# First expert in a place of 64 slots, heavy places between light ones, HGRN heads in pairs, score products in turns

## The chip, the cores and the metric

The kernel runs on one core of a Trainium2 chip. The core has a matrix engine (TensorE, PE in the profile), three engines for elementwise work (VectorE is DVE, ScalarE is ACT, GpSimd is POOL), and SyncE (SP), on whose queue nearly all weight loads are issued. PEld in the profile is TensorE's loading of the stationary operand. The metric is the device time of one execution in microseconds; less is better.

## The reference, cut to what matters

Two transformer blocks run in series over 256 tokens of width 1024, all in float32. The first has a mixer of four differential-attention heads and eight neighbourhood-attention heads, and a mixture of 32 experts of which each token takes 4. The second has two layers: layer 0 mixes by retention and NSA (the even mixer), layer 1 by HGRN2 (the odd mixer), and a dense SwiGLU follows each.

```python
# first block
o_diff = diff_attention(dq, dk, dv, lam, lam_init, g_subln)     # 4 heads, two score maps each
o_nat = neighbourhood_attention(nq, nk, nv, nat_rpb)            # 8 heads
x = x + gt1 * rms_norm(concat(o_diff, o_nat) @ w_out, g_post_mix)
h2 = rms_norm(x, g_pre_ffn) * (1 + sc2) + sh2
top_val, top_idx = top_k(h2 @ w_router + b_router, 4)
gates = softmax(top_val)
for e in range(32):                       # only the tokens that chose e
    y[e] = swiglu_clamped(h2[tok[e]] @ w1[e] + b1[e]) @ w2[e] + b2[e]     # w1: 8 MB, w2: 4 MB
x = x + gt2 * rms_norm(sum of gates * y, g_post_ffn)
# second block
x = x + retention_nsa_mixer(rmsnorm(x));  x = x + swiglu(rmsnorm(x))
x = x + hgrn2_mixer(rmsnorm(x));          x = x + swiglu(rmsnorm(x))
# hgrn2, per head: S_t = diag(f_t) S_{t-1} + k_t v_t^T ; o_t = S_t^T q_t      (8 heads, chunks)
```

With the given inputs the routing sends 33 tokens to expert 0. The other experts, sorted by load, have 93, 75, 62, 61, then 48 and less, and from about the middle of the list 32 and less.

## The kernel before

**Stages.** The first mixer runs until about 190 us of the trace, the experts from there to about 1170, and the second block to the end: even mixer, dense layer, odd mixer, dense layer.

**Places.** `experts()` works through 32 places in turn. Place 0 always holds expert 0, whose weights can be loaded before the routing is known. The other experts are sorted by load on the chip: `route()` computes their ranks and the one-hot matrix `PM`, a matrix product turns it into the row `ids` (which expert stands in which place), and SP reads an id from it by a TENSOR_LOAD before it issues that expert's loads. The table `SLOTS` fixes how many token slots each place has: 128, 64 or 32. The heaviest experts go to the 128-slot places, the lightest to the 32-slot ones.

**Work of a place.** Each expert has 12 weight tiles of 128x2048 float32: eight of w1 (`w1(p, dc)`) and four of w2. In a place of 64 or 32 slots the tile goes into the products as it is. In a place of 128 slots `split_e` divides each half tile into a high part (`ehi`, on ACT) and a low part (`elo`, on DVE), three products are summed, and the tokens are split likewise (`Xh`, `Xl`). The tokens of several places are gathered together by one-hot products (`gather`, tiles `oh` and `X`), and results are scattered back with gates (`scatter`, tile `macc`). The first three w1 steps of place p+1 stand ahead of the w2 steps of place p.

**Buffers.** Expert tiles rotate through 13 buffers of 1 MB (`tile_e`): eight in the pool `wp`, which the mixer's weights use too, and five in the pool `wx`, which opens when the mixer's pools close. Two more tiles of expert 0 (`w0`) lie in borrowed space.

**Order.** In `first_ffn` the order on PE and SP is the order of the code (`manual_schedule`). SP issues its loads strictly in turn, and a load that waits for a buffer holds up all behind it. On the other engines, and on all engines in the mixers, a scheduler sets the order.

**Score products.** `scores()` and its like in NSA compute for each head pair four products of 64 rows: two heads in the upper and lower half of the partitions (m or g), and two query halves (qt). Neighbouring products from different halves of the array can run at the same time; where the scheduler put both products of one half in a row, they do not.

**Odd mixer.** Each of the eight heads projects q and f (48 products `acc<-hh,whi` and the like, L91), then works through levels L = 1, 2, ... 128. At each level there is one small group of products (`ps_t<-qk`, 32x32) and one DVE multiplication (L1428) of the tile `qk`. Then come the products with `ip` (`ps_t<-ip,at`), ScalarE's square sums, a root on POOL, and the scaled copy to `on` (L1459). The PSUM banks are two of each kind, `s` and `t`, in rotation.

Of the kernel before, what the change touches and what calls it, by code (L numbers as in the profile page):

```python
# [31 lines left out]
class Block:  # L32
# [57 lines left out]
    def mm(self, out, lhsT, rhs, start, stop=False):  # L90
        self.nc.tensor.matmul(out, lhsT, rhs, start=start, stop=stop, skip_group_check=True)  # L91
# [249 lines left out]
    def first_mixer(self):  # L341
# [9 lines left out]

        self.norm_T(evac)
# [31 lines left out]
        def tm(g, fill=lambda: None):  # L384
            t = att.tile([128, 2, 512], F32, name=f"v{g}")
# [13 lines left out]
        ali = att.tile([128, 4, 384], F32, name="ali")  # L399
        nc.sync.dma_start(ali, A["alibi"])  # L400
# [19 lines left out]
        gt1 = att.tile([128, D], F32, name="gt1")  # L420
        prow = att.tile([128, 2, 512], F32, name="prow")
# [6 lines left out]
        for h in range(4):  # L428
# [3 lines left out]
            for m in range(2):  # L432
                P = att.tile([128, 2, T], F32, name="P", tag="P", bufs=4)
                for qt in range(2):
                    self.softmax_unit(P[:, qt], sps[m][:, qt], ali[:, h, 128 * (1 - qt):128 * (1 - qt) + 256],
                                      rs[:, m, qt:qt + 1])
# [87 lines left out]
    def scores(self, q, k):  # L524

        sps = [self.bank("s").rearrange("p (a k) -> p a k", a=2) for _ in range(2)]
        for qt in range(2):
            for m in range(2):
                r = slice(m * 64, m * 64 + 64)
                self.mm(sps[m][:, qt], q[r, qt * 128:qt * 128 + 128], k[r], start=(qt == 0), stop=(qt == 1))  # L530
# [94 lines left out]
    def places(self):  # L625
# [14 lines left out]
        self.placed = nc.vector.tensor_scalar(PM, self.rankof, rank, None, op0=OP.is_equal)  # L640
# [5 lines left out]
        nc.vector.tensor_copy(self.ids, pi[0:1, :NE])  # L646
# [80 lines left out]
    def gather(self, ps):  # L727
# [10 lines left out]
        for p in ps:  # L738
# [3 lines left out]
            if w == 128:  # L742
                Xh = self.moe.tile([128, ND, 2 * CAP], F32R, name="Xh")
# [13 lines left out]
        def part(q):  # L757
# [6 lines left out]
            for j in range(2):  # L764
                dc = 2 * q + j
                nc.scalar.activation(X[:, dc, :n], acc[:, j * 256:j * 256 + n], AF.Identity,
                                     bias=self.sh2[:, dc:dc + 1], scale=self.s2[:, dc:dc + 1])
            if Xh is not None:
                d = slice(2 * q, 2 * q + 2)
                self.last_act = nc.scalar.copy(Xh[:, d], X[:, d, big])  # L770
# [10 lines left out]
    def slot(self, k):  # L781
        if k < 8:
            return self.wp.tile([128, 2048], F32, name="w")
        return self.wx.tile([128, 2048], F32, name="w", tag=f"w{k}")
# [107 lines left out]
    def first_ffn(self):  # L892
        self.scratch = lambda: self.moe.tile([128, D], F32, name="scr", tag="Xh")
# [653 lines left out]
    def run(self):  # L1547
# [7 lines left out]
        if self.stop == 1:  # L1555
            return
# [178 lines left out]
```

## Time and profile before

| what | value |
|---|---|
| median of three runs | 1874.76 us (1873.25 to 1874.95) |
| the profiled execution | 1873.16 us |
| its span in the trace | 1871.6 us |
| first mixer | 0 to about 190 us |
| experts | about 190 to 1170 us |
| second block | about 1180 us to the end |

The profile page gives the busy share of each engine over the whole span; these are averages over stages with different limits. To see what bounds a stage, read a view of windows: for a stretch it gives the busy time of each engine, the granted clock of TensorE (PEclk, 1.00 is full speed, 2.4 GHz), the busy share of the DMA engines and the rate in GB/s. A timeline lists instructions by start time and duration, neighbours of one kind on one line with their count; in square brackets stands the idle time before, and what ended it. A view of waits sums the idle time by what ended it.

### The profile page before, as it was taken

What the parts mean: (1) busy time and instruction counts of PE and PEld (TensorE: products, weight loads), DVE (VectorE), ACT (ScalarE), POOL (GpSimd) and SP (SyncE); (2) the same over time, 40 slices, a digit from 0 to 9 for tenths busy, and PEclk for the clock granted to TensorE, in tenths of its full rate; (3) what the DMA queues carried; (4) which work ended last, traced back from release to release, by engine and by line L of the source; (5) the groups of instructions that cost most, each with busy time, mean ns of one, the idle gap of its engine ahead of it and who ended that gap; (6) DMA issues with size and microseconds to landing.
All of it is one profiled execution on the core that took longest, in us unless ns stands there. A gap on an engine that the chain in (4) does not pass through costs nothing. (4 is left out here: it accounts for less than half of the span.)

```text
span 1871.6 us, 27432 instructions
## 1 busy us (share of the span) xinstructions
PE 1726.3 (92%) x10671; PEld 1104.4 (59%) x10671; DVE 973.7 (52%) x1756; ACT 688.1 (37%) x1210; POOL 53.1 (3%) x101
## 2 busy tenths in 40 slices
PE   6999999999999899989986877899999999999998
PEld 4776653533543453453321211778899988779997
DVE  3535663653653563473321312577665658756655
ACT  3534551421432341351100101464544555554443
POOL 0000000000000000000000000200000001100000
PEclk8999999999999999989988878899999999999999
DMA  9784889999999999999999999723455543235530
GB/s 395 276 288 173 309 326 420 400 384 421 421 421 421 421 418 421 421 412 417 422 420 422 420 421 421 281 89 135 181 202 181 209 157 134 95 144 203 193 145 23
DMA packets 79990, 564.25 MB, mean 301 GB/s; under 512 B 8960, under 2 KB 9120, under 8 KB 13296
## 3 DMA queue, kind: packets, MB, share of 16 engines
q1 hardware_dynamic: 78800, 557.58, 74.8%
q0 software_dynamic: 1056, 4.87, 0.7%
q8 instruction: 86, 1.41, 0.3%
q14 instruction: 48, 0.39, 0.1%
HBM read 561.37 MB, written 1.05 MB: 301 GB/s over the span
## 5 line engine op out<-in xcount | busy, mean ns | idle before, releaser
L87 DVE TENSOR_TENSOR wlo<-w,whi 128x1024 fp32r<-128x1024 f32 (+1 forms) x232 | 281.1, 1215 | 191.3 <-ACT whi L86 190.9
L86 ACT CAST whi<-w 128x1024 fp32r<-128x1024 f32 (+1 forms) x232 | 241.0, 1044 | 317.1 <-PE acc L91 136.3
L91 PE MATMUL acc<-w,X 128*32 128x512 f32 (+1 forms) x1728 | 325.6, 633 | 28.2 <-DMA w<-in_w_dram 27.9
L91 PE MATMUL ps_s<-w,act 128*32 128x512 f32 (+1 forms) x864 | 164.6, 681 | 28.6 <-DMA w<-in_w_dram 24.1
L91 PEld LDWEIGHTS acc<-w,X 128*32 128x32 f32 (+1 forms) x1728 | 72.4, 124 | 191.9 <-issue 128.2
L798 DVE TENSOR_TENSOR elo<-w,ehi 128x1024 fp32r<-128x1024 f32 x120 | 145.4, 1222 | 31.2 <-ACT ehi L797 31.0
L888 DVE TENSOR_TENSOR macc<-macc,ps_t 128x512 f32<-128x512 f32 x124 | 84.5, 688 | 142.0 <-PE ps_t L91 141.9
L797 ACT CAST ehi<-w 128x1024 fp32r<-128x1024 f32 x120 | 124.8, 1050 | 63.5 <-PE acc L91 42.2
L877 DVE SCALAR_TENSOR_TENSOR yl<-ps_s,gslot,yh 128x512 fp32r<-128x512 f32 x37 | 27.3, 750 | 196.6 <-ACT yh L876 196.6
L91 PEld LDWEIGHTS ps_s<-w,act 128*32 128x32 f32 (+1 forms) x864 | 41.7, 128 | 129.1 <-issue 71.0
L91 PE MATMUL acc<-hh,whi 128*128 128x256 f32 x368 | 107.0, 291 | 2.0 <-ACT whi L86 2.0
L91 PE MATMUL acc<-hh,wlo 128*128 128x256 f32 x368 | 106.8, 290 | 0.5 <-DVE wlo L87 0.5
L91 PE MATMUL acc<-hl,whi 128*128 128x256 f32 x368 | 106.9, 290 | 0.0
L91 PE MATMUL ps_s<-hh,whi 128*128 128x256 f32 x352 | 98.6, 280 | 0.0
L91 PE MATMUL ps_s<-hl,whi 128*128 128x256 f32 x352 | 98.3, 279 | 0.0
L91 PE MATMUL ps_s<-hh,wlo 128*128 128x256 f32 x352 | 98.3, 279 | 0.0
L876 ACT ACTIVATE yh<-ps_s,gslot 128x512 fp32r<-128x512 f32 x37 | 24.9, 687 | 190.5 <-PE ps_s L91 190.5
L91 PE MATMUL ps_t<-hh,whi 128*128 128x256 f32 x320 | 89.4, 279 | 0.0
L91 PE MATMUL ps_t<-hl,whi 128*128 128x256 f32 x320 | 89.3, 279 | 0.0
L91 PE MATMUL ps_t<-hh,wlo 128*128 128x256 f32 x320 | 89.3, 279 | 0.0
L91 PEld LDWEIGHTS ps_t<-yh,ot 64*128 64x128 f32 (+1 forms) x128 | 23.6, 195 | 106.0 <-issue 60.4
L91 PEld LDWEIGHTS acc<-hh,whi 128*128 128x128 f32 x368 | 70.0, 190 | 9.2 <-issue 5.2
(426 smaller groups left out, 3246.6 us busy)
## 6 DMA issues: line engine op xcount, KB each, us to landing
w<-in_w_dram SPq DMA_DIRECT2D x384, 1024.0 KB, 19.5
w<-in_ffn_dram SPq DMA_DIRECT2D x66, 1024.0 KB, 4.8
w<-in_w_ada_dram SPq DMA_DIRECT2D x24, 1024.0 KB, 10.7
w<-in_w_in_dram SPq DMA_DIRECT2D x12, 1024.0 KB, 11.4
w<-in_even_cm_dram SPq DMA_DIRECT2D x8, 1024.0 KB, 16.6
w<-in_odd_qf_dram SPq DMA_DIRECT2D x8, 1024.0 KB, 4.8
w<-in_w_out_dram SPq DMA_DIRECT2D x4, 1024.0 KB, 7.9
w<-in_even_tm_dram SPq DMA_DIRECT2D x4, 1024.0 KB, 5.6
```

The lines of the kernel that those rows point to most:

```text
L86: nc.scalar.copy(hi[:, :n], w)
L87: nc.vector.tensor_tensor(lo[:, :n], w, hi[:, :n].bitcast(F32), op=OP.subtract)
L91: self.nc.tensor.matmul(out, lhsT, rhs, start=start, stop=stop, skip_group_check=True)
L797: self.nc.scalar.copy(hi, w)
L798: self.nc.vector.tensor_tensor(lo, w, hi.bitcast(F32), op=OP.subtract)
L876: nc.scalar.activation(yh[:, m], y, AF.Copy, scale=gs)
L877: nc.vector.scalar_tensor_tensor(yl[:, m], y, gs, yh[:, m].bitcast(F32), op0=OP.mult, op1=OP.subtract)
L888: nc.vector.tensor_tensor(self.macc[:, tt, m], self.macc[:, tt, m], q, op=OP.add)
```

## The change

- `SLOTS` comes from a written order: `F QQ FFQBQ FFFQBQ FFFQBQ FFFQBQ FFQQQQ`, with B for 128 slots, F for 64, Q for 32. Before, the order was `B QFFB QFFQB QFFFB QFFFB QFFF` and eight times Q. There are now 4 B, 14 F and 14 Q instead of 5, 13 and 14.
- Expert 0 stands in an F place. The early split of its first tile falls away, and the product for `ids` follows the first of four gather parts.
- A new pool `wy`, opened before the mixer's pools, holds two of the 13 expert buffers, and `Xh`. To make room, some of the mixer's tiles share a place (`ali` with `natb`, `prow` with `on`, `dv` with `nv`), and `gt1`, `scr`, `gt2` share with `Xh`. The 13 buffers are used in plain rotation.
- `in_turns` fixes that score products of the two row halves alternate.
- `hgrn_pair` works on two heads at a time: one DVE multiplication per level for both, small groups of both heads next to each other.

```diff
-BIGS, FULLS = (0, 4, 9, 14, 19), (2, 3, 6, 7, 11, 12, 13, 16, 17, 18, 21, 22, 23)
-SLOTS = [128 if p in BIGS else 64 if p in FULLS else 32 for p in range(NE)]
+ORDER = "F QQ FFQBQ FFFQBQ FFFQBQ FFFQBQ FFQQQQ".replace(" ", "")
+SLOTS = [{"B": 128, "F": 64, "Q": 32}[k] for k in ORDER]
...
+    def in_turns(self, calls):
+        last = None
+        for args in calls:
+            with self.tc.issue_after(last.ins) if last else nullcontext():
+                last = self.mm(*args)
...
     def tile_e(self):
-        k = ([*range(6), *range(8, 13), 6, 7, *range(6)] + [12, *range(6, 12), *range(6)] * NE)[self.nload]
+        k = (11, 12, 8, 9, 10, *range(8))[self.nload % 13]
...
             places = self.places()
             next(places)
-            last_oh = self.placed
-            with self.tc.issue_after(last_oh.ins), self.tc.issue_after(self.last_sq.ins):
-                self.halves += [self.split_e(wl[0][:, m * 1024:m * 1024 + 1024]) for m in range(2)]
-            for k, step in enumerate(rest):
+            rest.pop(0)()
+            next(places)
+            for step in rest:
                 step()
-                if k == 1:
-                    next(places)
...
+        for h0 in range(0, 8, 2):
+            self.hgrn_pair(h0, hh, hl, ip, on, hm, ATs)
...
+        pcs = [self.bank("t")[:, :384].rearrange("p (a l n) -> p a l n", a=2, l=6) for _ in range(2)]
+        pls = [self.bank("s").rearrange("p (a n) -> p a n", a=4) for _ in range(2)]
+        def small(lv, Q):
+            for i in range(2):
                 for tt in range(2):
                     for b in range(4):
-                        c = slice(tt * 128 + b * 32, tt * 128 + b * 32 + 32)
-                        self.mm(pc[b * 32:b * 32 + 32, tt, lv], ks[:, c], Q[:, c], start=True, stop=True)
+                        c = slice(i * T + tt * 128 + b * 32, i * T + tt * 128 + b * 32 + 32)
+                        self.mm(pcs[i][b * 32:b * 32 + 32, tt, lv], ks[:, c], Q[:, c], start=True, stop=True)
...
-            nb = T // (2 * L)
-            v = qk[:, L:2 * T - L].rearrange("p (w k l) -> p w k l", w=2, l=L)[:, :, ::2]
+            nb = 2 * T // (2 * L)
+            v = qk[:, L:4 * T - L].rearrange("p (w k l) -> p w k l", w=2, l=L)[:, :, ::2]
...
+            self.wy = c.enter_context(tc.tile_pool(name="wy", bufs=1))
+            with ExitStack() as b:
+                self.sp = b.enter_context(tc.tile_pool(name="sp1", bufs=2))
+                self.att = b.enter_context(tc.tile_pool(name="att1", bufs=1))
```

DVE's row before, around the ranks of the experts in `route()`: `PM` is the one-hot of the ranks, `ids` the row that SP reads, `elo` the low part of expert 0's first tile.

```order
L638 TENSOR_SCALAR rank_1759<-rank_1759,c0_73 32x1
L640 TENSOR_SCALAR PM_1762<-c0_73,rank_1759 32x32
L798 TENSOR_TENSOR elo_1765<-w0_1716,ehi_1764 128x1024
L798 TENSOR_TENSOR elo_1769<-w0_1716,ehi_1768 128x1024
L771 TENSOR_TENSOR Xl_1749<-X_1747,Xh_1748 128x256 x2
L646 CAST ids_1792<-ps_s_1790 1x32
```

The same place on DVE now.

```order
L646 TENSOR_SCALAR rank_1762<-rank_1762,c0_73 32x1
L648 TENSOR_SCALAR PM_1765<-c0_73,rank_1762 32x32
L654 CAST ids_1776<-ps_s_1774 1x32
L658 TENSOR_SCALAR st4_1695<-v8_1691 128x1 x2
L339 TENSOR_TENSOR adarows_1591<-adarows_1591,prow2_1719 128x512
```

The two splits and two `Xl` differences that stood between `PM` and `ids` are gone.

PE's row now, from the gather of place 0 to the end of its w1 steps: `oh` with `x` are the gather products, `acc_1799` collects place 0, `w_1928` is place 1's first tile.

```order
L91 MATMUL ps_s_1774<-PM_1765,c0_73 1x32
L91 MATMUL ps_t_1778<-oh_1751,x_70 128x64 x4
L91 MATMUL ps_t_1785<-oh_1751,x_70 128x64 x4
L91 MATMUL ps_t_1792<-oh_1751,x_70 128x64 x4
L91 MATMUL acc_1799<-w0_1721,X_1752 64x512 x4
L91 MATMUL acc_1799<-w0_1722,X_1752 64x512 x4
L672 MATMUL ps_t_1821<-c0_73,pos_1710 32x128 x2
L672 MATMUL ps_t_1825<-c0_73,G_1690 32x128 x2
L91 MATMUL ps_s_1829<-PM_1765,posT_1820 128x32 x2
L91 MATMUL ps_s_1829<-PM_1765,GT_1819 128x32 x2
L91 MATMUL acc_1799<-w_1725,X_1752 64x512 x4
L91 MATMUL acc_1799<-w_1727,X_1752 64x512 x4
```

PE's row before, for one tile of place 0: each half tile takes three pairs of products with the split parts.

```order
L91 MATMUL acc_1812<-ehi_1826,Xh_1748 128x512 x2
L91 MATMUL acc_1812<-ehi_1826,Xl_1749 128x512 x2
L91 MATMUL acc_1812<-elo_1827,Xh_1748 128x512 x2
L91 MATMUL acc_1813<-ehi_1836,Xh_1748 128x512 x2
L91 MATMUL acc_1813<-ehi_1836,Xl_1749 128x512 x2
L91 MATMUL acc_1813<-elo_1837,Xh_1748 128x512 x2
```

A tile is now read by four products straight from its buffer, which those products free; before, the buffer was freed by the splits, and PE had twelve products a tile.

PE's row in the odd mixer before, at the step from one head to the next: `ps_t_12037` takes the products with `ip` of one head, `ps_t_12121` the next head's level groups.

```order
L91 MATMUL acc_12229<-hh_11687,whi_12258 128x256
L91 MATMUL acc_12229<-hl_11688,whi_12258 128x256
L91 MATMUL acc_12229<-hh_11687,wlo_12259 128x256
L91 MATMUL ps_t_12037<-ip_11738,at0_11675 128x128 x3
L91 MATMUL ps_t_12121<-qs_12113,qk_12114 32x32 x8
L91 MATMUL ps_t_12121<-qk_12114 32x32 x8
```

The same engine now, at the step from one pair to the next; of the twelve `acc` rows between, the last three are shown in the second fence.

```order
L91 MATMUL ps_s_11814<-qk_11675 128x128
L91 MATMUL acc_12325<-hl_11488,whi_12331 128x256
L91 MATMUL acc_12325<-hh_11487,wlo_12332 128x256
L91 MATMUL acc_12325<-hh_11487,whi_12331 128x256
L91 MATMUL ps_t_11958<-ip_11538,at0_11475 128x128 x3
L91 MATMUL ps_t_11986<-ip_11538,at1_11477 128x128 x3
L91 MATMUL acc_12325<-hl_11488,whi_12331 128x256
```

```order
L91 MATMUL acc_12325<-hl_11488,whi_12359 128x256
L91 MATMUL acc_12325<-hh_11487,wlo_12360 128x256
L91 MATMUL acc_12325<-hh_11487,whi_12359 128x256
L91 MATMUL ps_t_12134<-qs_12004,qk_12005 32x32 x8
L91 MATMUL ps_t_12134<-qk_12005 32x32 x8
```

The two `ip` products of a pair take both `t` banks, and the next pair's first level group `ps_t_12134`, which needs the first of these banks again, now has twelve products between; before, the next head's group had the other bank and followed at once.

## Rows read from the trace of the kernel before

**Rows 1.** The profile page's first line.

```profile
span 1871.6 us, 27432 instructions
```

**Rows 2.** Windows by stage: from:to, length, engines' busy (count), clock, DMA share, GB/s.

```profile
0.00:190.00 190.00, 168.99 (x1014) 118.03 (x1015) 88.76 (x207) 81.40 (x171) 9.02 (x21) 0.97 0.74 283
1180.00:1275.00 95.00, 93.92 (x811) 81.50 (x812) 66.20 (x208) 49.77 (x125) 2.63 (x5) 0.97 0.41 149
1550.00:1660.00 110.00, 105.25 (x1366) 84.25 (x1365) 83.20 (x184) 56.56 (x148) 19.23 (x41) 1.00 0.34 116
```

**Rows 3.** Windows within the expert stage, same columns.

```profile
214.00:290.00 76.00, 72.00 (x381) 42.87 (x382) 50.53 (x93) 36.47 (x57) 1.31 (x4) 1.00 0.87 330
350.00:400.00 50.00, 46.51 (x238) 29.09 (x238) 35.72 (x51) 23.90 (x34) 0.00 (x0) 1.00 0.94 366
400.00:650.00 250.00, 234.65 (x1110) 105.70 (x1107) 115.96 (x192) 71.31 (x115) 0.00 (x0) 0.98 1.01 421
950.00:1150.00 200.00, 148.72 (x777) 34.35 (x769) 44.99 (x100) 19.74 (x52) 0.00 (x0) 0.78 1.01 421
1150.00:1167.00 17.00, 11.86 (x69) 3.12 (x68) 4.87 (x11) 1.54 (x5) 0.00 (x0) 0.87 1.01 422
```

**Rows 4.** Timeline of PE at the last place's end: start, duration, instruction.

```profile
1167.26 1.06 PE L91 MATMUL ps_s<-w,act 128*32 128x512 f32 x8 [1.22 <-DMA w<-in_w_dram]
```

**Rows 5.** The page's DMA issues: count, KB each, median us from issue to landing.

```profile
w<-in_w_dram SPq DMA_DIRECT2D x384, 1024.0 KB, 19.5
w<-in_ffn_dram SPq DMA_DIRECT2D x66, 1024.0 KB, 4.8
```

**Rows 6.** Timeline of SP's queue from place 1 on: first issue, stretch, count.

```profile
209.34 268.96 SPq L790 DMA_DIRECT2D w<-in_w_dram  x105
```

**Rows 7.** Timeline of DVE from the ranks to the ids.

```profile
203.11 0.23 DVE L640 TENSOR_SCALAR PM<-c,rank 32x32 f32<-32x32 f32 x1
203.26 2.34 DVE L798 TENSOR_TENSOR elo<-w,ehi 128x1024 fp32r<-128x1024 f32 x2
208.02 0.17 DVE L646 CAST ids<-ps_s 1x32 int32<-1x32 f32 x1
```

**Rows 8.** Timeline of PE in place 0, and in a place of 64 slots (last row).

```profile
201.85 3.78 PE L91 MATMUL ps_t<-oh,x 128*128 128x128 f32 x16 [0.53 <-DVE oh L753]
215.41 0.64 PE L664 MATMUL ps_t<-c,G 128*32 128x128 f32 x2 [1.34 <-DVE G L656]
227.27 0.98 PE L91 MATMUL ps_t<-oh,x 128*128 128x32 f32 x8
567.69 3.65 PE L91 MATMUL acc<-w,X 128*64 128x512 f32 x16
```

**Rows 9.** Groups of instructions from 950 to 1150 us: count | busy, mean ns | idle before.

```profile
L91 PE MATMUL acc<-w,X 128*32 128x512 f32 x416 | 67.1, 728 | 26.4 <-DMA w<-in_w_dram 26.4
L91 PE MATMUL ps_s<-w,act 128*32 128x512 f32 x224 | 45.5, 899 | 23.3 <-DMA w<-in_w_dram 22.9 <-DVE go L860 0.3
L91 PE MATMUL ps_t<-yh,ot 64*128 64x512 f32 x25 | 14.7, 638 | 1.5 <-DVE macc L888 1.5
```

**Rows 10.** Timeline of PE at NSA's score products.

```profile
1220.67 0.97 PE L91 MATMUL ps_s<-KS,nq 64*128 64x144 f32 x8
1228.25 0.97 PE L91 MATMUL ps_s<-KS,nq 64*128 64x144 f32 x4
```

**Rows 11.** Timelines of PE and ACT in the odd mixer, at one head's end.

```profile
1570.94 0.37 PE L91 MATMUL acc<-hh,wlo 128*128 128x256 f32 x1
1571.15 0.28 PE L91 MATMUL acc<-hh,whi 128*128 128x256 f32 x1
1571.26 0.28 PE L91 MATMUL acc<-hl,whi 128*128 128x256 f32 x1
1572.06 0.91 PE L91 MATMUL ps_t<-ip,at 128*128 128x128 f32 x6 [0.28 <-ACT at L1446]
1575.31 0.63 ACT L1459 ACTIVATE on<-ps_t,hrr 128x128 f32<-128x128 f32 x2 [1.50 <-POOL hrr L1457]
```

More of the change, by code (lines that the diff above doesn't have):

```diff
@@ L1 @@
 import math
-from contextlib import ExitStack
+from contextlib import ExitStack, nullcontext
 import numpy as np
@@ L90, in mm @@
     def mm(self, out, lhsT, rhs, start, stop=False):
[L91 removed]
+        return self.nc.tensor.matmul(out, lhsT, rhs, start=start, stop=stop, skip_group_check=True)
+    def in_turns(self, calls):
[3 more added lines that the diff above has]
+                last = self.mm(*args)
     def rms_scale(self, ss, n, eps, name):
@@ L398, in first_mixer @@
         dk = cm(1, 1.0)
-        ali = att.tile([128, 4, 384], F32, name="ali")
-        nc.sync.dma_start(ali, A["alibi"])
+        ali = []
+        for k in range(2):
+            ali.append(att.tile([128, 2, 384], F32, name="ali", tag="natb", bufs=2))
+            nc.sync.dma_start(ali[k], A["alibi"][:, 2 * k:2 * k + 2])
         lamv = self.small.tile([64, 4], F32, name="lamv")
@@ L526, in scores @@
         sps = [self.bank("s").rearrange("p (a k) -> p a k", a=2) for _ in range(2)]
[L527 to L530, printed above, removed]
+        rs = [slice(m * 64, m * 64 + 64) for m in range(2)]
+        self.in_turns([(sps[m][:, qt], q[rs[m], qt * 128:qt * 128 + 128], k[rs[m]], qt == 0, qt == 1)
+                       for qt in range(2) for m in range(2)])
         return sps
@@ L1412, in odd_mixer @@
+        small(0, qs)
+        tot = f
+        lv = 1
+        L = 1
+        while L <= 128:
+            if L <= 16:
+                small(lv, qp)
+            for i in range(2):
+                if L == 32:
                     for tt in range(2):
                         for b in range(2):
-                            c = tt * 128 + b * 64
-                            self.mm(pl[b * 64:b * 64 + 32, tt, b * 64 + 32:b * 64 + 64], ks[:, c:c + 32],
+                            c = i * T + tt * 128 + b * 64
+                            self.mm(pls[i][b * 64:b * 64 + 32, tt, b * 64 + 32:b * 64 + 64], ks[:, c:c + 32],
@@ new lines, in hgrn_pair @@
+                        self.mm(pls[i][0:64, tt, 64:128], ks[:, c:c + 64], qp[:, c + 64:c + 128], start=True, stop=True)
+                if L == 128:
+                    c = i * T
+                    self.mm(pls[i][:, 2], ks[:, c:c + 128], qp[:, c + 128:c + 256], start=True, stop=True)
+            if L == 128:
+                break
+            nb = 2 * T // (2 * L)
+            v = qk[:, L:4 * T - L].rearrange("p (w k l) -> p w k l", w=2, l=L)[:, :, ::2]
+            tv = tot.rearrange("p (b two) -> p two b", two=2)
@@ L1434, in odd_mixer @@
+            nc.vector.tensor_tensor(v, v, tv[:, :, :, None].to_broadcast([128, 2, nb, L]), op=OP.mult)
+            nt = att.tile([128, nb], F32, name=f"tot{L}", bufs=2)
+            nc.vector.tensor_tensor(nt, tv[:, 0], tv[:, 1], op=OP.mult)
+            tot = nt
+            L *= 2
+            lv += 1
+        for i in range(2):
+            h = h0 + i
+            hs = slice(h * 128, h * 128 + 128)
+            pc, pl = pcs[i], pls[i]
             tm = att.tile([128, 2, 6, 32], F32, name="tm", bufs=2)
```

136 lines of the change are left out of this document (57 added, 79 removed).

## The prediction

> **What bounds the kernel now.** I read the windows by stage first. In the first mixer PE is busy 169 of 190 us; in the even mixer 93.9 of 95 and in the odd mixer 105 of 110 [rows 2], so there every microsecond of PE work counts nearly in full. In the expert stage the reader should look at the last column: from 400 us on the DMA engines move 421 GB/s, with PE busy only 149 of 200 us in the last part [rows 3], and the very last group of expert products waits for its weight tile [rows 4]. So the stage ends when the last of 384 tiles of 1024 KB has landed [rows 5]. At 421 GB/s a tile (1.049 MB) takes 2.49 us and a place of 12 tiles 29.9 us. What can be gained there is only time in which this stream did not run at full rate. I read where that was: place 1's loads begin only at 209.34 [rows 6], and the rate is 330 GB/s from 214 to 290 and 366 from 350 to 400 [rows 3]. That is 76 x (1 - 330/421) = 16.4 us and 50 x (1 - 366/421) = 6.5 us of lost stream.
>
> **The change part by part.**
>
> *The ids come earlier.* Before, DVE has `PM` done at 203.34, then two splits, together 2.34 us, stand in its row, and `ids` is written at 208.02 [rows 7]; SP issues 1.32 us later [rows 6]. Now the splits are gone and the ids product follows the first gather part. That part is the first half of the 16 entries that take 3.78 us from 201.85 [rows 8], so it is over by 203.7 even at the old width. I put the copy at 203.9, so SP at 205.2: **4.1 us** earlier. A load into an idle queue takes 4.8 us to land [rows 5], so place 1's first tile lands at 210.0 instead of 214.1.
>
> *Place 0 frees its buffers faster.* Three buffers are free for place 1; every later load waits until a w1 step of place 0 has read its tile. Before, DVE and ACT had to split each tile. Now four products read it, 3.65 us for two tiles, 1.83 each [rows 8]. I follow PE: the 16 gather products, 32 entries of between 0.12 us (the 32-column ones, 0.98 for 8) and 0.24 us (the 128-column ones) [rows 8], at 0.165, end near 207.2. Two tiles of w1: 210.9. Then the gate transposes, which before waited for `G` until 215.41 [rows 8], behind the casts of the splits on ACT; with those gone I take 212.2 and some 2 us for them and the products behind: 214.3. The six tiles left take 11.0 us, the four gather parts of place 1 between them 3.9 (0.98 each), the bias products about 1.7: 230.9. The ninth load waits for that last tile and lands 4.8 later, at 235.7; a stream without a gap would have it at 210.0 + 8 x 2.49 = 229.9. So **5.8 us** stay lost where 16.4 were: a gain of **10.6**. The following loads wait for w1 steps of place 1, a light one, and the stream has no reason to stop again. Ends: nothing gained here (0) and the gap fully closed (16.4); I stay near the middle because each step has its row.
>
> *The light places beside the heavy ones.* The loss from 350 to 400 falls on the first heavy place after place 0. From 400 to 650 the same five places (one heavy, three full, one light) go by at 421 GB/s [rows 3], so their work fits into 5 x 29.9 = 149.5 us. The new cycle of six has one light place more. In the stretch of light places at the end, such a place has 64 entries of w1 and 32 of w2, 64/416 x 67.1 + 32/224 x 45.5 = 16.8 us, and at most 4.7 for its scatter (twice 4/25 x 14.7) [rows 9]: 21.5. So six places need at most 171.0 us of PE where the stream needs 179.3. I take the **6.5 us** as gained, ends 0 and 6.5. After place 0 nothing else in the stage gains, since the stream is already full: one heavy place fewer is worth nothing by itself.
>
> Sum for the stage: 4.1 + 10.6 + 6.5 = 21.2 us.
>
> *Score products in turns.* In NSA, eight entries that alternate between the halves take 0.97 us, while four of one half alone take the same 0.97 [rows 10]. So a set written half by half takes 1.94. There are eight such sets (KS and KW for four head pairs), and one alternated already. In the new order most sets have their first product alone and the other three in a row, which I put at 0.33 + 0.1 + 0.97; 7 x 0.5 = 3.5, and I take **3 us** with PE full [rows 2]. Ends: 7 x 0.97 = 6.8, and a loss of 1 by other products moved. The eight sets of the first mixer are partly alternated and PE has 21 us of idle time there [rows 2]: **1 us**, from 4 gained to 3 lost, the latter if the shared places of `ali`, `prow` and `v` make a load or copy wait.
>
> *Odd mixer by pairs.* Behind a small group the next product starts 0.21 us later (1570.94 to 1571.15), otherwise 0.11 (1571.15 to 1571.26) [rows 11]: 0.10 for the switch. Pairs halve the groups: 8 levels x 4 pairs = 32 switches, 3.2 us. Against that stands a new wait. The next pair's first level group needs the bank in which the products with `ip` were; before it took the other bank. From those products' start to the end of the scaled copy is 1572.06 to 1575.94, 3.9 us [rows 11]; in between PE has the second head's products (0.91) and twelve others (12 x 0.11), 2.2 us. That leaves 1.7 at each of three pair steps, 5.1 us; behind it on PE's queue is all of the next projection. The halved number of DVE multiplications gives perhaps 1 back. Net **1 us lost**; ends 4 gained (no stall), 8.5 lost (3 x 3.9 - 3.2, no cover at all).
>
> The Trainium skill (TensorEngine Tiling (Array Packing), Key Properties) says that a change of the tiling mode drains TensorE, without a price. The 0.10 us above is what the trace shows for it; were the drain hidden here, pairs would save nothing and the net would be 4 us lost, the time some 3 us later.
>
> Total: 21.2 + 1 + 3 - 1 = 24.2 us. The profiled execution took 1873.16 us (span 1871.6 [rows 1]), 1.6 below the median of 1874.76. 1873.16 - 24.2 = 1849.0; on the median's footing **1850.5 us**.
>
> **The rivals.**
>
> (a) *The pair step is uncovered.* If all 3.9 us show at three steps, the odd mixer loses 8.5 instead of 1: 1858. For it: ScalarE has two heads' squares and copies in a row there, with casts between. Against: the scheduler put twelve products there. 0.14.
>
> (b) *The start stays as it is.* If something else than the splits holds place 0's buffers (the gate chain on POOL and ACT, the swiglu), only the ids' 4.1 and the 6.5 come: 1850.5 + 10.6 = 1861. For it: PE too was busy 72 of 76 us there [rows 3], so splits and products were close. Against: PE's work for place 0 falls to four products a tile. 0.10.
>
> (c) *All goes well.* The stream starts with a gap of 1 instead of 5.8, NSA gains 6.8, the pair steps cost nothing: 4.8 + 3.8 + 5 better, 1837. 0.05.
>
> (d) *PE falls behind in the expert stage, and the kernel gets slower.* The light places make PE wait, and its granted clock drops: 0.98 from 400 to 650, but 0.78 and 0.87 where PE waits for tiles [rows 3], between the levels of 1.2 and 2.4 GHz. If PE went into each heavy place like that, the cycle's 171.0 us would stretch by 0.98/c. It outgrows the stream's 179.3 at c = 0.93; four cycles lose the whole gain (6.1 us each) at c = 0.90. At 0.87 it is 192.6, four times 13.3 more: 1904. Against: the stretch with 0.78 still runs at 421 GB/s, and heavy places keep PE busy. 0.04.
> The Trainium skill (TensorE: Matmul & The Clock Gate, section HAM oscillation — how this bites in real kernels) tells of just this, a matrix engine that waits for weights, is throttled, and starts its next work cold. The clock of 0.78 in the stretch of light places agrees; that it reaches a heavy place no row shows.
>
> That an overflow path is taken (expert 0 with over 64 tokens) is excluded by its 33 tokens.
>
> **How the numbers follow.** Forecast 0.65 (1844 to 1856), (a) 0.14, (b) 0.10, (c) 0.05, (d) 0.04; 0.02 for a start gain and a mixer loss that cancel. The range from 1839 to 1862 takes in (a) and (b) and leaves out (c), (d) and the rest. Faster or slower means by over 0.2%, 3.7 us, about what a measurement of this kernel can tell from no change. Faster: 0.65 + 0.14 + 0.10 + 0.05 = 0.94, less 0.01 for tails. Same 0.03, slower 0.04.
>
> **What would show it.** `ids` written near 204 and place 1's first issue near 205; a rate over 380 GB/s from 214 to 290; 421 from 350 to 400; the last expert products near 1146 instead of 1167. In NSA, sets of score products under 1.5 us. In the odd mixer, idle time of PE before `ps_t<-qs,qk`, released by `on`. I am wrong if the rate sags at places 6, 12, 18 and 24 (then (d)), or if the stage ends at 1155 or later with place 0 slow (then (b)).

## The result, and the profile after

The changed kernel takes 1850.31 us in the median (four runs, 1847.63 to 1851.33), the kernel before 1874.86 on the same chip. The ratio is 0.9862, with a 95% interval of 0.984 to 0.9885: about 25 us faster. The profiled execution has a span of 1846.0 us, 25.6 us shorter than [rows 1].

Where the time went is read from the starts of the stages on PE (the timeline of PE: start, duration, instruction). The first row is the last place's last group of expert products; then come the first transposes of `x` at the head of the even mixer, its dense layer, the odd mixer and its dense layer. The kernel after:

```profile
1144.80 1.06 PE L91 MATMUL ps_s<-w,act 128*32 128x512 f32 x8 [1.42 <-DMA w<-in_w_dram]
1157.80 0.45 PE L159 MATMUL ps_t<-c,x 128*128 128x128 f32 x1 [7.18 <-ACT whi L86]
1305.39 0.49 PE L159 MATMUL ps_t<-c,x 128*128 128x128 f32 x3
1493.46 0.27 PE L159 MATMUL ps_t<-c,x 128*128 128x128 f32 x1
1648.82 0.49 PE L159 MATMUL ps_t<-c,x 128*128 128x128 f32 x3
```

The kernel before (its last place's products are in [rows 4]):

```profile
1180.50 0.45 PE L152 MATMUL ps_t<-c,x 128*128 128x128 f32 x1 [7.43 <-DVE x L555]
1326.80 0.60 PE L152 MATMUL ps_t<-c,x 128*128 128x128 f32 x4
1514.86 0.27 PE L152 MATMUL ps_t<-c,x 128*128 128x128 f32 x1
1674.26 0.49 PE L152 MATMUL ps_t<-c,x 128*128 128x128 f32 x3
```

The differences give the balance. The expert stage ends 22.5 us earlier (1167.26 to 1144.80). The even mixer takes 147.6 instead of 146.3 us: 1.3 lost, of which 1.1 lie behind its first NSA score product (see the score products below). The first dense layer is the same (188.1). The odd mixer takes 155.4 instead of 159.4: 4.0 gained. The rest is within 0.3.

What the windows of the expert stage show, with the columns of [rows 3]:

```profile
214.00:290.00 76.00, 71.27 (x424) 27.59 (x422) 22.95 (x58) 15.41 (x36) 0.00 (x0) 0.98 1.00 403
350.00:400.00 50.00, 43.05 (x222) 26.42 (x220) 35.98 (x56) 27.58 (x42) 0.00 (x0) 1.00 1.01 420
```

Against [rows 3] the rate from 214 to 290 rose from 330 to 403 GB/s and the sag from 350 to 400 (366) is gone. DVE's timeline at the ends of the mixer and of the routing, in the kernel after, and below it the row of the kernel before that answers to the first:

```profile
182.89 1.41 DVE L563 SCALAR_TENSOR_TENSOR x<-agt,agr,x 128x512 f32<-128x512 f32 x2
198.54 0.23 DVE L648 TENSOR_SCALAR PM<-c,rank 32x32 f32<-32x32 f32 x1
199.52 0.18 DVE L654 CAST ids<-ps_s 1x32 int32<-1x32 f32 x1 [0.75 <-PE ps_s L91]
```

```profile
186.61 1.40 DVE L555 SCALAR_TENSOR_TENSOR x<-agt,agr,x 128x512 f32<-128x512 f32 x2
```

So the mixer itself ends 3.7 us earlier, `PM` 4.6 us earlier [rows 7], and `ids` 8.5 us earlier, 1.0 behind `PM` instead of 4.9.

### The profile page after: what moved, and what is told of

The parts are those of the page before. It is cut to its first block, busy times and chain, and to the rows that moved or that the text cites. A ratio compares the mean times of both kernels' runs of the same rounds, so it can differ in the third digit from the quotient of the medians.

```text
span 1846.0 us, 27219 instructions
## 1 busy us (share of the span) xinstructions
PE 1692.1 (92%) x10647; PEld 1079.7 (58%) x10647; DVE 931.6 (50%) x1661; ACT 661.5 (36%) x1186; POOL 53.6 (3%) x101
## 5 line engine op out<-in xcount | busy, mean ns | idle before, releaser
L91 PE MATMUL acc<-w,X 128*64 128x512 f32 (+1 forms) x1792 | 338.6, 622 | 28.8 <-DMA w<-in_w_dram 28.5
L86 ACT CAST whi<-w 128x1024 fp32r<-128x1024 f32 (+1 forms) x232 | 241.0, 1045 | 325.1 <-PE acc L91 147.1
L91 PE MATMUL ps_s<-w,act 128*64 128x512 f32 (+1 forms) x896 | 167.4, 640 | 34.9 <-DMA w<-in_w_dram 30.1
L91 PEld LDWEIGHTS acc<-w,X 128*64 128x64 f32 (+1 forms) x1792 | 76.2, 124 | 198.7 <-issue 124.0
L806 DVE TENSOR_TENSOR elo<-w,ehi 128x1024 fp32r<-128x1024 f32 x96 | 116.2, 1221 | 20.3 <-ACT ehi L805 18.8
L91 PEld LDWEIGHTS ps_s<-w,act 128*64 128x64 f32 (+1 forms) x896 | 42.3, 126 | 139.3 <-issue 72.0
L805 ACT CAST ehi<-w 128x1024 fp32r<-128x1024 f32 x96 | 99.9, 1049 | 49.1 <-PE acc L91 31.1
L774 ACT ACTIVATE X<-ps_t,sh,s 128x224 f32<-128x224 f32 (+4 forms) x88 | 38.4, 486 | 109.4 <-PE ps_t L91 108.5
```

The source lines that it names most:

```text
L86: nc.scalar.copy(hi[:, :n], w)
L91: return self.nc.tensor.matmul(out, lhsT, rhs, start=start, stop=stop, skip_group_check=True)
L774: self.last_act = nc.scalar.activation(X[:, dc, :n], acc[:, j * 256:j * 256 + n], AF.Identity, bias=self.sh2[:, dc:dc + 1], scale=self.s2[ ...
L805: self.nc.scalar.copy(hi, w)
L806: self.nc.vector.tensor_tensor(lo, w, hi.bitcast(F32), op=OP.subtract)
```

## The experiments

Each number below is read against the kernel before on the same chip. The intervals of the ratios are about 0.2% to either side, so differences of 1 to 4 us between kernels are read in the stages of their traces. Five of the kernels below have the changed kernel's expert stage unaltered behind the same mixer (the changed kernel itself, its second run, and the runs on the heads, on the s banks and on NSA). In them the last expert tile lands between 1144.8 and 1146.2 us: that is the spread of this stage. Two more stretches vary between kernels in which they are the same. From the first transposes of the even mixer to NSA's first score product it takes 40.2 to 43.7 us: 40.4 in the changed kernel at a granted clock of 0.77 in the first 10 us, 43.7 in the run with work in the wait at 0.50. The odd mixer by pairs takes 155.4 or 156.8 us (see the last runs). With the spread of the expert stage, that is why several spans came out 2 to 5 us above what was expected before the run, and why no verdict below rests on a span alone.

### The places alone

The kernel before with the new table, expert 0 in 64 slots and no early split. The marker `last_act`, which orders work behind the gather, moves from the copy to `Xh`, which place 0 no longer makes, to the copy to `X` (not shown).

```diff
-BIGS, FULLS = (0, 4, 9, 14, 19), (2, 3, 6, 7, 11, 12, 13, 16, 17, 18, 21, 22, 23)
+ORDER = "F QQ FFQBQ FFFQBQ FFFQBQ FFFQBQ FFQQQQ".replace(" ", "")
...
-            with self.tc.issue_after(last_oh.ins), self.tc.issue_after(self.last_sq.ins):
-                self.halves += [self.split_e(wl[0][:, m * 1024:m * 1024 + 1024]) for m in range(2)]
```

> The kernel before with the new order of places alone: expert 0 in 64 slots and no early split, no new pool, the ids product where it was, score products and odd mixer as before. Theory A (the place of expert 0 is what makes the stage shorter; it frees the buffers in time): the rate from 214 to 290 us rises from 330 to about 400 GB/s, the sag from 350 to 400 goes, the last tile lands some 17 to 19 us earlier, span about 1853. Theory B (the earlier loads through the new pool are needed too, since the first tiles land late): about half, span 1862.

Ratio 0.9886 (0.9863 to 0.9910), span 1853.0 us. Its last place's products on PE, and its windows:

```profile
1148.24 1.06 PE L90 MATMUL ps_s<-w,act 128*32 128x512 f32 x8 [0.75 <-DMA w<-in_w_dram]
214.00:290.00 76.00, 70.85 (x430) 28.07 (x428) 25.41 (x68) 15.41 (x36) 0.00 (x0) 0.98 0.95 386
350.00:400.00 50.00, 45.52 (x236) 28.62 (x232) 32.54 (x49) 25.49 (x37) 0.00 (x0) 1.00 1.01 421
```

The stage ends at 1148.24 instead of 1167.26: 19.0 of the 22.5 us come from the table. Theory A holds; the pool's early loads are not needed for it. Of the 19.0 us, 10.1 lie between 214 and 290 (330 to 386 GB/s) and 6.5 between 350 and 400. Some 2 more lie between 650 and 950, where the stream ran at 418 GB/s before and now runs at 421. This run changes place 0 and the order behind it together, so it does not tell which of the two removed the sag from 350 to 400.

### Place 0 heavy again

The changed kernel with the first B and the first F exchanged, so that the counts stay.

```diff
-ORDER = "F QQ FFQBQ FFFQBQ FFFQBQ FFFQBQ FFQQQQ".replace(" ", "")
+ORDER = "B QQ FFQFQ FFFQBQ FFFQBQ FFFQBQ FFQQQQ".replace(" ", "")
```

> The changed kernel with place 0 at 128 slots and the first heavy place behind it at 64, so that the numbers of places of each kind stay the same; the first tile is not split early. Theory A (the start is faster because place 0 frees its buffers without the splits): the rate from 214 to 290 us falls from 403 back to 330 to 350 GB/s, and all behind comes some 10 us later: span about 1856. Theory B (the earlier ids and the buffers of the new pool made the start faster): the rate stays near 400, the span 1846 to 1848.

Ratio 1.0006 (0.9996 to 1.0016): all the gain is gone (span 1872.7 us), and more than the expected 10 us. The last expert tile lands at 1169.9 instead of 1144.8. The window, and from DVE's timeline the first and the last of place 0's 24 splits, two a tile:

```profile
214.00:290.00 76.00, 68.16 (x356) 43.67 (x360) 46.50 (x87) 33.20 (x51) 0.00 (x0) 0.93 0.72 265
```

```profile
205.97 1.23 DVE L806 TENSOR_TENSOR elo<-w,ehi 128x1024 fp32r<-128x1024 f32 x1 [0.27 <-ACT ehi L805]
265.64 1.23 DVE L806 TENSOR_TENSOR elo<-w,ehi 128x1024 fp32r<-128x1024 f32 x1 [0.17 <-ACT ehi L805]
```

The splits of the 12 tiles take from 205.97 to 266.87, 5.1 us a tile, where the full stream brings a tile in 2.49. A tile's buffer is free only behind its splits, and the stream brings 265 GB/s. Earlier ids and the new pool, which this kernel has, change nothing in that. Which kind of place comes first decides the start, and is worth 25 us of the stage in this order.

### The ids behind the whole gather

```diff
-            rest.pop(0)()
-            next(places)
             for step in rest:
                 step()
+            next(places)
```

> The changed kernel with the ids product behind all four parts of the gather instead of behind the first. Place 1's first load then begins some 5.4 us later (206.3 instead of 200.9). Theory A (the prediction's step: the stream starts with the ids, 4.1 us of its start are worth 4.1 us): the last expert tile lands some 5 us later, the span is about 1851. Theory B (only three buffers are free; the fourth load waits for place 0's third w1 step until 213.2 in any case, and the ids have slack): nothing moves by more than 1 us, span 1845.5 to 1847.

Ratio 0.9871 (0.9855 to 0.9887). DVE's timeline, and PE at the last place:

```profile
204.84 0.18 DVE L654 CAST ids<-ps_s 1x32 int32<-1x32 f32 x1 [5.86 <-PE ps_s L91]
```

```profile
1145.96 1.06 PE L91 MATMUL ps_s<-w,act 128*32 128x512 f32 x8 [0.59 <-DMA w<-in_w_dram]
```

The ids come 5.3 us later, the rate from 214 to 290 stays at 403 GB/s, and the stage ends within its spread. Theory B in the stage (the span, 1849.9, is longer than it said, mostly by the two stretches that vary): three loads find a free buffer, and the fourth waits for place 0's third w1 step, whether the first three were issued at 201 or at 206. The ids have slack.

### Without the early loads through the new pool

```diff
-        k = (11, 12, 8, 9, 10, *range(8))[self.nload % 13]
+        k = (8, 9, 10, 11, 12, *range(8))[self.nload % 13]
```

> The changed kernel with the two buffers of the new pool last instead of first in the rotation, so that only expert 0's two borrowed tiles are loaded before the mixer's pools close, and its other ten from about 167 us on. Theory A (the last of the twelve tiles lands at 191.9 us and is read from 205 on; five microseconds later costs nothing): span within 1 us of 1846 or, with the clock's spread, up to 1850; the stage's last tile within 1 us of 1144.8. Theory B (the pool's early loads carry part of the gain): the last tile 3 to 5 us later.

Ratio 0.9867 (0.9845 to 0.9890). Expert 0's last tile lands at 197.2 instead of 191.9 us, the stage's last tile at 1146.1, within the spread. Theory A, with the reservation that 1.4 us of the profiled run is about as much as can be told apart.

### Place 1's gather behind place 0's w1 steps

The same work on PE in another order, so that place 0's buffers are read earlier.

```diff
-                if dc > 3:
-                    flush(2)
+                if dc == 7:
+                    biases = self.biases()
+                    next(biases)
+                    flush(3)
+                    next(biases)
+                    flush()
```

> The changed kernel with the bias products and the gather of place 1 behind the last w1 step of place 0 instead of between its steps: the same work on TensorE in another order. In the trace of the changed kernel place 0's last w1 tile is read at 227.7 us and the ninth load of the following stream lands at 234.9. Theory A (the reads of place 0's tiles set when the stream can start): that tile is read at about 222, the ninth load lands near 230.5, the last expert tile 3 to 4 us earlier than 1144.8, the span about 1842.5. Theory B (the next loads, which wait for place 1's first steps, come no earlier, so that the stream only stops later): the last tile stays within 1 us of 1144.8 to 1146.

Ratio 0.9867 (0.9846 to 0.9887). PE's timeline: the last six w1 steps of place 0, the first of place 1, and the last place:

```profile
213.43 10.52 PE L91 MATMUL acc<-w,X 128*64 128x512 f32 x48
230.37 1.94 PE L91 MATMUL acc<-w,X 128*32 128x512 f32 x8
1147.42 1.06 PE L91 MATMUL ps_s<-w,act 128*32 128x512 f32 x8 [0.84 <-DMA w<-in_w_dram]
```

Place 0's tiles are read out by 224, as meant, but the next buffer becomes free only with place 1's first step, which now ends at 232.3. The stop moved by one load, and the stage ends 1.2 us above its spread. That is theory B in kind, though the last tile at 1147.4 lies 0.4 us beyond its bound. What counts is PE's work up to place 1's first steps, not its order.

### Work for PE in the wait for the routing mask

```diff
+        spin = self.bank("t")
+        for k in range(4):
+            with self.tc.issue_after(lt.ins):
+                self.mm(spin, self.ident, self.x[:, 0, 0:512], start=True, stop=True)
```

> The changed kernel with four added 128x512 products (1.84 us by the rate of its weight products, result unused) in the 2.1 us in which TensorE waits for the routing mask. The granted clock is 0.65 from 195 to 200 and 0.50 from 200 to 205 us there; the 24 gather entries behind take 5.38 us and the first two w1 steps 4.63 instead of 3.65. Theory A (the idle 2.1 us are what lets the clock fall, and the slow clock delays place 0, which holds the buffers): the gather takes 3 to 4 us, the first two w1 steps 3.7, the last expert tile lands 2 to 3.5 us earlier, span 1842.5 to 1844. Theory B (the small matrix products of the routing let it fall, not the wait): clock and span stay, or the span grows by up to 0.5 us.

Ratio 0.9874 (0.9847 to 0.9901). Windows of 5 us of the changed kernel (the column before the last two is the granted clock), then of this one with PE's first two w1 steps:

```profile
195.00:200.00 5.00, 4.19 (x27) 3.75 (x27) 3.01 (x16) 0.67 (x2) 0.00 (x0) 0.65 0.00 0
200.00:205.00 5.00, 5.00 (x25) 4.88 (x26) 0.42 (x1) 1.59 (x6) 0.00 (x0) 0.50 0.59 210
```

```profile
195.00:200.00 5.00, 4.01 (x29) 2.79 (x27) 2.61 (x13) 0.56 (x2) 0.00 (x0) 0.98 0.00 0
200.00:205.00 5.00, 5.00 (x25) 4.91 (x24) 1.59 (x5) 1.53 (x5) 0.00 (x0) 0.50 0.45 146
205.40 5.92 PE L91 MATMUL acc<-w,X 128*64 128x512 f32 x16
```

The clock stayed near 1.00 until 200, but fell to 0.50 (1.2 GHz) all the same, and the 24 gather entries take 5.38 us as before. The first two w1 steps take 5.92 us against the 4.63 of the changed kernel (shown below). That can't be put down to this edit: the runs on the ids and on the gather's order take 6.2 and 6.0 there without it. Theory A falls. The added products ran longer than was put down, 3.70 us instead of 1.84, so the mask's first product starts 1.4 us later than in the changed kernel. The span, 1850.8, is 4.8 us longer, where theory B allowed 0.5: 1.3 by the last expert tile (1146.1, within the spread), 3.3 at the head of the even mixer. That the small products of the routing make the clock fall, as theory B says, was not tested by itself.

### The score products

Left to the scheduler everywhere:

```diff
         for args in calls:
-            with self.tc.issue_after(last.ins) if last else nullcontext():
-                last = self.mm(*args)
+            self.mm(*args)
```

> The changed kernel with its score products left to the scheduler again, as before. In the trace of the changed kernel the first mixer's last addition to x begins at 182.9 instead of 186.6 us, and the even mixer takes 147.6 instead of 146.3 us. Theory A (the turns do both: they gain 3.7 us in the first mixer and lose 1.3 in the even one): the addition goes back to about 186.6, the even mixer to 146.3, the span from 1846.0 to about 1848.4. Theory B (the first mixer's gain comes from elsewhere, the shared places or the loads): the addition stays at 182.9, the even mixer goes to 146.3, the span to about 1844.7. The prediction's own step (turns gain 1 and 3 us) would give 1850.

Ratio 0.9874 (0.9858 to 0.9891), span 1850.2. DVE's timeline at the end of the first mixer:

```profile
186.24 1.41 DVE L562 SCALAR_TENSOR_TENSOR x<-agt,agr,x 128x512 f32<-128x512 f32 x2
```

The mixer ends 3.35 us later than in the changed kernel and the expert stage 4.4 later (its last tile lands at 1149.2, 3.0 above the spread). So nearly all that the first mixer gained is due to the turns: theory A there. In every run with turns the addition begins between 182.1 and 183.5, in those without between 185.9 and 186.6. For the even mixer neither theory's 146.3 came. It takes 147.1, of which 106.1 lie behind NSA's first score product, as in the kernel before; the rest is its head, one of the two stretches that vary.

Left to the scheduler in NSA alone:

```diff
-                self.in_turns(todo)
+                for args in todo:
+                    self.mm(*args)
```

> The changed kernel with NSA's score products left to the scheduler, and those of the first mixer still in turns. From NSA's first score product to the end of the even mixer the kernels with turns took 107.2 us, those without 106.1. Theory A (in NSA the turns cost 1.1 us, because the first product of a set runs ahead alone and TensorE changes over more often): 106.1 us again, first mixer unchanged (the addition to x at 182 to 183 us), span 1845 if the clock does not dip in the odd mixer. Theory B (the order of the later fillers differs for another reason): 107.2.

Ratio 0.9857 (0.9836 to 0.9877). PE's timeline of this kernel, its first score product and the end of the even mixer:

```profile
1200.10 0.97 PE L91 MATMUL ps_s<-KS,nq 64*128 64x144 f32 x8
1306.22 0.49 PE L159 MATMUL ps_t<-c,x 128*128 128x128 f32 x3
```

The changed kernel's first score products, and one set each with KW and KS:

```profile
1198.15 0.97 PE L91 MATMUL ps_s<-KS,nq 64*128 64x144 f32 x8
1200.04 0.46 PE L91 MATMUL ps_s<-KW,nq 64*128 64x128 f32 x2
1202.85 0.92 PE L91 MATMUL ps_s<-KW,nq 64*128 64x128 f32 x6
1205.53 0.51 PE L91 MATMUL ps_s<-KS,nq 64*128 64x144 f32 x2
1208.52 0.73 PE L91 MATMUL ps_s<-KS,nq 64*128 64x144 f32 x4
1209.99 0.72 PE L91 MATMUL ps_s<-KS,nq 64*128 64x272 f32 x2
```

That is 106.1 us without turns and 107.2 with them (1198.15 to 1305.39): in NSA the turns cost 1.1 us. Theory A. The last five rows show where the prediction's price held and where it didn't. The first product of a KW set goes ahead alone (0.46), the other three follow 2.8 us later (0.92): 1.38 us, as priced. A KS set comes in three pieces that sum to 1.96, no less than half by half. Without turns, on the other hand, the scheduler twice put half of one set beside half of the next (1.24 us for both halves). Together the sets' products took 12.0 us with turns and 12.8 without. That saves 0.8. But PE's busy time in the stretch stays the same (105.6 and 105.5 us), so other products take the 0.8 back; the sets stand in 17 groups instead of 13, but that this is the reason is not shown. And PE is idle 1.7 us instead of 0.7: a wait of 0.8 for DVE's `raw` and one of 0.2 for `nm` are new, and they are the 1.1 us lost.

### The heads of the odd mixer

One by one again, by the loop of the kernel before:

```diff
-        for h0 in range(0, 8, 2):
-            self.hgrn_pair(h0, hh, hl, ip, on, hm, ATs)
+        scale = 128 ** -0.5
+        for h in range(8):
...
```

> The changed kernel with the odd mixer's heads one by one again. It took 155.4 us by pairs and 159.4 before. Theory A (pairs as such save 4.0 us, although TensorE waits some 5.9 us at the pair steps): the odd mixer takes 159.4 again, the span is about 1850.0. Theory B (the prediction's step: pairs lose 1 us net, and something else made the stage shorter): it takes 154.4 or 155.4, the span 1845 to 1846.

Ratio 0.9880 (0.9864 to 0.9897). PE's timeline, the ends of its odd mixer, and a level group of one head with the products next to it:

```profile
1495.53 0.27 PE L159 MATMUL ps_t<-c,x 128*128 128x128 f32 x1
1654.87 0.49 PE L159 MATMUL ps_t<-c,x 128*128 128x128 f32 x3
1545.79 0.33 PE L91 MATMUL ps_t<-qk 128*32 128x32 f32 x16
1546.05 0.39 PE L91 MATMUL acc<-hl,whi 128*128 128x256 f32 x1
1546.28 0.28 PE L91 MATMUL acc<-hh,wlo 128*128 128x256 f32 x1
1546.40 0.28 PE L91 MATMUL acc<-hh,whi 128*128 128x256 f32 x1
```

It takes 159.3 us, theory A: pairs are worth 4.0 us. In the changed kernel the same view shows a pair step with its waits, and a level group of two heads:

```profile
1553.69 0.33 PE L91 MATMUL ps_t<-qs,qk 128*32 128x32 f32 x16 [0.99 <-ACT on L1496]
1555.38 0.33 PE L91 MATMUL ps_t<-qs,qk 128*32 128x32 f32 x16 [0.79 <-ACT qk L1421]
1556.57 0.28 PE L91 MATMUL acc<-hh,whi 128*128 128x256 f32 x1
1556.78 0.46 PE L91 MATMUL ps_t<-qk 128*32 128x32 f32 x32
1557.17 0.38 PE L91 MATMUL acc<-hl,whi 128*128 128x256 f32 x1
```

The first two pair steps cost 1.8 us of waiting each, the third 2.3: 5.9 in all. Of these 3.1 were released by `on` (0.99 + 0.99 + 1.08), the rest by `qk` and `qs`. The windows of the two odd mixers, one by one first, then the changed kernel's:

```profile
1495.53:1654.87 159.34, 154.15 (x1636) 125.16 (x1635) 110.41 (x220) 82.00 (x182) 21.56 (x46) 1.00 0.40 137
1493.46:1648.82 155.36, 146.55 (x1636) 122.75 (x1634) 103.83 (x164) 81.50 (x182) 22.78 (x46) 1.00 0.40 141
```

By pairs PE is busy 7.6 us less and idle 3.6 more (8.8 instead of 5.2): 4.0. The groups explain the 7.6: one head's group holds the products back by 0.26 us, two heads' group by 0.39 (1556.78 to 1557.17), not 0.52. The product ahead of a group takes 0.21 instead of 0.12 to the next start, and the one behind 0.10 more as well, as the prediction had it. One group less saves 0.13 + 0.09 + 0.10, about 0.3 us, and the `acc` products are interrupted 24 times less in the stage (52 instead of 76): some 8 us, an estimate that agrees with the 7.6.

The products with `ip` in other banks:

```diff
-            po = self.bank("t").rearrange("p (a e) -> p a e", a=4)
+            po = self.bank("s").rearrange("p (a e) -> p a e", a=4)
```

> The changed kernel with the products with ip written to the s banks instead of the t banks, so that the next pair's first level group needs no bank that they use. In the trace of the changed kernel TensorE waits 5.9 us at the three pair steps. Theory A (the bank is the cause): these waits go, the odd mixer takes about 149.5 to 150.5 instead of 155.4 us, span 1840 to 1841. Theory B (the wait is the length of the chain through ScalarE and GpSimd and comes back at the level that needs the s banks): the odd mixer stays within 1.5 us of 155.4.

Ratio 0.9858 (0.9835 to 0.9882). The odd mixer takes 155.6 us. From PE's timeline at the second pair step:

```profile
1576.05 0.33 PE L91 MATMUL ps_t<-qs,qk 128*32 128x32 f32 x16 [2.37 <-DVE qs L1422]
1577.50 0.41 PE L91 MATMUL acc<-hh,wlo 128*128 128x256 f32 x1
```

The wait for the bank is gone, but `qs` is late there instead, for its sigmoid stands on ScalarE behind the copies to `on` and a weight cast. Idle PE in the stage falls only from 8.8 to 7.3 us. And behind the wait of 2.37 the clock falls: the products take 0.41 instead of 0.28, at a granted clock of 0.83 in the 10 us from 1575.2. PE's busy time in the stage is 1.7 us longer, which uses up what the shorter waits gave. Theory B, in a form that was not foreseen.

### Three edits together, and the changed kernel once more

The edits of the gather's order, of NSA and of the s banks, as shown above, in one kernel:

> Three edits on the changed kernel together: place 1's gather behind place 0's w1 steps, NSA's score products left to the scheduler, the odd mixer's products with ip in the s banks. Theory A (each does what the single runs showed): 3.5 + 1.1 + 0 to 1.5 us less than the changed kernel, span 1840 to 1842, some 5 us under the changed kernel on the same chip. Theory B (the clock's spread at the start of the even mixer and at the pair steps covers it): within 2 us of the changed kernel.

The changed kernel without an edit:

> The changed kernel once more, for the comparison on the same chip and for the spread between executions: a median of 1848 to 1851 us. Theory A (the clock dips at a pair step of the odd mixer in some executions and not in others): the profile shows the odd mixer at 155.4 us with a granted clock of 1.00 throughout, or at 156.8 with 0.83 in one stretch of 10 us. Theory B: the odd mixer takes another time than these two.

Ratios 0.9862 (0.9840 to 0.9884) and 0.9865 (0.9843 to 0.9887): the same. The three edits shorten the even mixer to 146.7 us, but their expert stage ends with a last tile at 1148.5, 2.3 us above the spread, which is in the direction of the run with the gather moved. That is theory B. No version here beats the changed kernel; the one with NSA left alone is 0.6 us lower in the median, inside the intervals.

The second run of the changed kernel shows the odd mixer at 155.4 us and a clock of 1.00. Five others with the same odd mixer (place 0 heavy, ids late, no early loads, gather moved, NSA left alone) take 156.8 or 156.9. The windows at the first pair step, ids late first, then the changed kernel:

```profile
1557.00:1567.00 10.00, 9.28 (x203) 8.43 (x204) 6.62 (x10) 3.59 (x7) 0.00 (x0) 0.83 0.08 14
```

```profile
1555.00:1565.00 10.00, 9.62 (x229) 8.71 (x230) 8.33 (x13) 4.08 (x7) 0.10 (x1) 1.00 0.27 91
```

A dip of the clock behind the two waits of a pair step goes with 1.4 us more. The runs with the score products left alone and with work in the wait have the same odd mixer too, at 155.4 and 155.3 us and a clock of 1.00. The two executions of the changed kernel agree, so theory A's words (in some executions and not in others) hold between kernels with the same odd mixer; between executions of one kernel it is not shown, and what decides it stays open.

## Why the prediction was right, and where its steps were not

The total was right: 1850.5 forecast, 1850.31 measured. What bounds the kernel was right too: the stream of tiles in the expert stage, which place 0 held up. But that the total is so close is luck. The places were put 2.2 us too high (21.2 for 19.0) and NSA 4.1 too high (3 gained for 1.1 lost); the first mixer was put about 2.5 too low (1 for 22.5 - 19.0 = 3.5) and the odd mixer 5.0 too low (1 lost for 4.0 gained). These nearly cancel.

**The expert stage, 21.2 forecast.** The table of places alone gave 19.0, and place 0's kind decides the start. But the split into terms was wrong. The ids' 4.1 us are worth nothing by themselves, because the fourth load waits for place 0 in any case; that run shows that I added two conditions of which only the later counts. That place 0 has three buffers ahead and then holds the stream stood in the prediction; I did not ask which of the two comes last. With the ids out, the gain of 10.6 + 6.5 was a little low against 19.0. With the table alone the loss from 214 to 290 fell from 16.4 to 76 x (1 - 386/421) = 6.3 us, 10.1 gained for 10.6, and the 6.5 us from 350 to 400 came as forecast. That nothing else in the stage gains was wrong: from 650 to 950 the stream had lost 300 x (1 - 418/421), some 2 us, and those came as well. In the changed kernel, where the mixer ends 3.7 us earlier, the loss from 214 to 290 is 76 x (1 - 403/421) = 3.2 us.

The followed path of PE was close in sum and wrong in parts. PE's timeline in place 0 of the changed kernel (the rest of the gather, the first two w1 steps, the last of place 0 with the first of place 1):

```profile
199.41 5.38 PE L91 MATMUL ps_t<-oh,x 128*128 128x64 f32 x24
204.72 4.63 PE L91 MATMUL acc<-w,X 128*64 128x512 f32 x16
225.76 2.93 PE L91 MATMUL acc<-w,X 128*64 128x512 f32 x16
```

Place 0's last tile is read at 227.7, 3.2 us before the forecast 230.9, because the mixer ended earlier. The steps themselves were slower: the gather has 0.22 us an entry where I took 0.165, and two w1 steps take 4.63 instead of 3.65. The clock is at 0.50 to 0.83 there.

**The first mixer, 1 forecast.** 3.7 by the end of the mixer, of which the turns make 3.35. I priced the products alone. Those take 14.4 us in sum instead of 16.3 in the run without turns, and PE's waits shrink as well: from 66 us to the mixer's end it is idle 2.2 instead of 3.9 us, and the wait for the softmax's `nm` (1.3 us) is gone. The shared places of `ali`, `prow` and `v` cost nothing to be seen.

**NSA, 3 forecast.** 1.1 lost. The step that failed is the saving of 0.5 for each of seven sets. The price of the lone first product held (1.38 for a KW set, 1.43 forecast), but the KS sets fell into three pieces and saved nothing. The sets without turns did not take 1.94 each either, 12.8 in all instead of 0.97 + 7 x 1.94 = 14.6. And PE waits 1.0 us more, which I put at nothing.

**The odd mixer, 1 lost by forecast.** 4.0 gained. The stall was right in size, 5.1 forecast and 5.9 measured, but not in its cause: the bank, which `on` releases, ended 3.1 us of it, and with the bank out of the way PE waits for `qs` and `qk` instead. The gain by fewer groups was mis-sized: I counted the 0.10 behind a group, 3.2 us in all, and left out that PE is slower into a group too and that two heads' small products side by side take less than twice one head's. PE is busy 7.6 us less.

**The rivals.** (a), the uncovered pair step, has 5.9 us of the 11.7 that it supposed. (b) did not come, and of (c) neither the gain in NSA nor the free pair steps. (d) did not come either: from 400 to 950 the stream runs at 421 GB/s at a clock of 0.97. The Trainium skill's rule that was weighed there (TensorE: Matmul & The Clock Gate, section HAM oscillation — how this bites in real kernels: a matrix engine that waits is throttled and starts cold) may show at another place: in five runs the clock falls to 0.83 behind the waits of a pair step, though in four others with nearly the same waits it stays at 1.00. In place 0 it is 0.50, but the run with the wait filled shows that there the wait ahead was not the cause by itself.

## What to carry to other kernels

Where a stream of loads is the bound, look at what holds its buffers when it starts: here one place that had to split its tiles, put first, cost 25 us of the stream, while the four such places later, among lighter ones, let it run at 421 GB/s from 400 to 950 us. Two conditions for the same start don't add up; find out which is met last before either is priced. An order that was forced on small products paid in the first mixer, where the engine waited for their result, and cost 1.1 us in NSA, where the engine was full, the sets came in more pieces and it had to wait elsewhere.

## What was not expected of the hardware

The granted clock fell to 0.50 for 5 to 10 us in the gather of place 0 although PE was busy 5.00 of 5.00 us there. Ahead of it PE had waited 2.14 us for the routing mask and then worked on small products; the clock fell too when that wait was filled with work (0.98, then 0.50), and the kernel before has 0.50 from 200 to 205 us as well. What makes it fall stays open. In five of the runs that have the changed odd mixer the clock dipped to 0.83 at a pair step behind waits of only 0.99 and 0.79 us, in the others it did not. And a heavy place 0 without the early split of its first tile is slower than the kernel before had it: 265 GB/s from 214 to 290 us against 330. No run adds the early split alone, so that it is the cause is not shown.
